# The convolution branch in four token-stationary groups: gate products made tokens first, turned by TensorE, taps channels first

## The chip, the core and the metric

The kernel runs on one core of a Trainium2 chip. The metric is the device time of one execution in microseconds; "before" is the median of three executions. Engines are named as in the profile: PE (TensorE, matmuls; PEld its weight loads), DVE (VectorE), ACT (ScalarE), POOL (GpSimd) and SP (SyncE, here a queue of DMAs alone).

## What is computed

One residual block over 512 tokens of width 2048: a projection of the normalised input into three branches (gated short convolution, latent attention, attention into a memory of 256 tokens) and merge gates, a projection of each branch, and an output projection. The change concerns the first branch:

```python
h = rms_norm(x, norm_g[l])
proj = h @ w_in[l]
(c_gate, b_gate, u, conv_z, ...) = jnp.split(proj, split_at, axis=-1)   # 1024 columns each
conv_y = b_gate * causal_depthwise_conv(c_gate * u, conv_w[l])          # 3 taps along the tokens
o_conv = (conv_y * jax.nn.silu(conv_z)) @ w_conv_out[l]
```

So 4096 of the columns of `w_in` make four arrays of 512 tokens by 1024 channels. Two are multiplied and filtered along the tokens, and the result is multiplied by the other two, one of them after SiLU. Everything is float32.

## The kernel before

**Matmuls.** Each float32 operand is cut into a high and a low part (`split`: ACT writes the high part, line 117, DVE the difference, line 119), and each product is three matmuls, high by high, high by low, low by high (`mm3`, lines 127 to 129). Large products are done by a two-by-two scheme with seven block products instead of eight, named P1 to P7 (P1, P7, P5, P6, P4, P3, P2 here); a step is one of these block products for one piece of the contraction. Sums and differences of weight blocks that a product needs are made by DVE in place in the loaded tile (`raw`, lines 306, 311, 366). The block forms of the input `BX` are made once and stay.

**Two kinds of group.** `f_group` holds 512 output columns with the weights stationary: PE loads a 128x128 block of weights and 256 tokens move through (128x256 rows in the profile). The result has channels on the partitions. A group has 14 steps of 24 matmuls. `t_group` holds 1024 output columns with the tokens stationary: 512 columns of weights move through (128x512 rows). The result has tokens on the partitions. A group has 28 steps of 12 matmuls. Both have 336 matmuls. `f_results` and `t_results` take the block products out of PSUM as they come and hand finished blocks on, for a `t_group` to `put(t, n, r)` (three of the four quarters; t the half of the tokens, n the half of the columns) and `direct` (the fourth, straight from PSUM, after P2).

**Order.** All groups append to one list, `steps`; `run_range` issues the matmuls of a step, then the forms (high and low parts) of the next step's weights, then what was hung behind the step with `after`. The order of instructions on PE, DVE, ACT and POOL is then set by a scheduler, within the dependencies; each engine runs its own list in order. SP's queue keeps the order written. Weights are loaded by `fetch` into a ring of ten tiles, up to eight loads ahead; high and low parts sit in a ring of six tiles (`wf`), so three steps' worth. Working tiles come from a pool of 19 (`q`), of which twelve hold block forms of the input through this stage. PSUM is two sets of four banks, `acc` and `aux`; a `t_group` uses all eight, X and W in `acc`, Y and Z in `aux`.

**The stage of the change.** One gate group (a `t_group` whose results go through a sigmoid and to DRAM), then eight `f_group`s for the convolution, each with 128 channels of all four arrays, then another gate group, four more `f_group`s, and so on. `conv_group` takes each group's results, channels on the partitions: DVE multiplies two (`cu`, L637), ACT makes the first tap (L639), DVE the others (L640, L641) and two more products (L642, L643), and the result is stored (L644). The tap weights are one number per channel, so here one per partition.

**Turning.** `transpose4` (L143) turns four 128x128 blocks by PE into one PSUM bank. In the last part of the program, `turn` does that for the merged rows.

Of the kernel before, what the change touches and what calls it, by code (L numbers as in the profile page):

```python
# [19 lines left out]
AF = mybir.ActivationFunctionType  # L20
# [3 lines left out]
P = 128  # L24
# [67 lines left out]
def body(ctx, tc, a, out):  # L92
# [70 lines left out]
    def g(col):  # L163
        return gains[:, col:col + 1]
# [30 lines left out]
    def q(name, dtype=F32):  # L195
        return work.tile([P, 2, 512], dtype, tag="q", name=name, bufs=NQ)
# [15 lines left out]
    def flat(t):  # L212
        return t.rearrange("p k n -> p (k n)")
# [405 lines left out]
                consume(0, sc["r0"])  # L619
        return results  # L620

    cus = []

    def conv_group(cb):
        keep = {}

        def consume(half, r):
            if not cus:
                cus.append(flat(q("cu"))[:, :S + 2])
                vec.memset(cus[0][:, :2], 0.0)  # L630
            cu = cus[0]
            if half:
                keep["bz"] = r
                act.activation(r[:, 1], r[:, 1], AF.Silu)
                return
            bz, cv = keep["bz"], r[:, 0]
            vec.tensor_tensor(out=cu[:, 2:], in0=r[:, 0], in1=r[:, 1], op=ALU.mult)  # L637
            wc = G_CONV + 3 * cb
            act.activation(cv, cu[:, 0:S], AF.Copy, scale=g(wc))  # L639
            vec.scalar_tensor_tensor(out=cv, in0=cu[:, 1:S + 1], scalar=g(wc + 1), in1=cv, op0=ALU.mult, op1=ALU.add)  # L640
            vec.scalar_tensor_tensor(out=cv, in0=cu[:, 2:S + 2], scalar=g(wc + 2), in1=cv, op0=ALU.mult, op1=ALU.add)  # L641
            vec.tensor_tensor(out=cv, in0=cv, in1=bz[:, 0], op=ALU.mult)  # L642
            vec.tensor_tensor(out=cv, in0=cv, in1=bz[:, 1], op=ALU.mult)  # L643
            nc.scalar.dma_start(adram[8 + cb], cv)  # L644
        return f_results(consume)

    def z_group(d, n0):
        def consume(half, r):
            act.activation(flat(r), flat(r), AF.Silu)
            nc.scalar.dma_start(two(d, n0 + 2 * half), r)  # L650
        return f_results(consume)

    def t_results(put, direct, early=None, add=None):


        sc, seen = {}, set()

        def results(name, bk):
            seen.add(name)
            if name in ("P1", "P7"):  # L660
                k, slot = ("u", "X") if name == "P1" else ("v", "Y")
                sc[k] = q(k)
                for tt in range(2):
                    act.activation(sc[k][:, tt], bk[slot][tt], AF.Copy)
                if early and name == "P7":
                    early(1, 1)
            u, v = sc.get("u"), sc.get("v")
            if name == "P5":
                for tt in range(2):
                    vec.tensor_tensor(out=v[:, tt], in0=bk["Z"][tt], in1=v[:, tt], op=ALU.add)  # L670
                if add:
                    vec.tensor_tensor(out=flat(v), in0=flat(v), in1=flat(add(1, 1)), op=ALU.add)
                if early:
                    early(0, 1)
            if name == "P6":
                for tt in range(2):
                    vec.tensor_tensor(out=u[:, tt], in0=bk["W"][tt], in1=u[:, tt], op=ALU.add)
                r = q("r")
                vec.tensor_tensor(out=flat(r), in0=flat(u), in1=flat(v), op=ALU.add)
                put(1, 1, r)  # L680
                if early:
                    early(1, 0)
            if name in ("P4", "P6") and seen >= {"P4", "P6"}:
                r = q("r")
                for tt in range(2):
                    vec.tensor_tensor(out=r[:, tt], in0=bk["Y"][tt], in1=u[:, tt], op=ALU.add)
                if add:
                    vec.tensor_tensor(out=flat(r), in0=flat(r), in1=flat(add(0, 1)), op=ALU.add)
                    vec.tensor_tensor(out=flat(u), in0=flat(u), in1=flat(add(1, 0)), op=ALU.add)
                put(0, 1, r)  # L690
                if early:
                    early(0, 0)
            if name == "P2":
                direct(bk["X"], q("r"))
            if name == "P3":
                r = q("r")
                for tt in range(2):
                    vec.tensor_tensor(out=r[:, tt], in0=bk["Z"][tt], in1=u[:, tt], op=ALU.add)
                put(1, 0, r)
        return results  # L700
# [21 lines left out]
    def gate_group(b, grp, lead=False):  # L722
        t_group(a[("w_gmem", "w_gconv", "w_gmla")[b]][grp], BX, rows_group(gdram[b], grp, AF.Sigmoid), lead)

    gate_group(0, 0, True)
    for cb in range(8):
        f_group(a["w_conv"][cb], BX, conv_group(cb), "aux" if cb % 2 else "acc")
    gate_group(0, 1)
    for grp in range(4):
        f_group(a["w_mlaz"][grp], BX, z_group(zdram, 4 * grp), "aux" if grp % 2 else "acc")  # L730
    gate_group(1, 0)
# [690 lines left out]
def two_by_two(w, cols, near=False):  # L1422

    w = np.concatenate([w[:, c0:c0 + n] for c0, n in cols], axis=1)
    if near:
        w = w.reshape(8, 2, P, 512).transpose(1, 0, 2, 3)
    w = w.reshape(2, 2, 4, P, 2, HS)
    w = np.stack([w[k, :, :, :, n] for k, n in ((0, 0), (0, 1), (1, 1), (1, 0))])  # L1430
    return np.ascontiguousarray(w.transpose(0, 1, 3, 2, 4)).reshape(8, P, 4 * HS)


def two_by_two_t(w, near=False):

    if near:
        w = w.reshape(8, 2, P, 1024).transpose(1, 0, 2, 3)
    w = w.reshape(2, 4, 2, P, 2, 512)  # L1440
    w = np.stack([w[k, :, :, :, n] for k, n in ((0, 0), (0, 1), (1, 1), (1, 0))])
    return np.ascontiguousarray(w.transpose(0, 1, 3, 2, 4)).reshape(16, P, KC * 512)
# [6 lines left out]
def layout(inp):  # L1449
    i = {k: np.asarray(v) for k, v in inp.items()}  # L1450
    w_in = i["w_in"][0]
    a = {}
    a["memT"] = np.ascontiguousarray(i["mem"][0].reshape(M, KB, P).transpose(2, 1, 0))
    a["xT"] = np.ascontiguousarray(i["x"][0].reshape(S, KB, P).transpose(2, 1, 0))
    a["pos"] = np.ascontiguousarray(i["positions"][0].reshape(NTB, P).T)
    cw = i["conv_w"][0].reshape(3, 8, P).transpose(2, 1, 0).reshape(P, 24)
    a["gains"] = np.ascontiguousarray(np.concatenate(
        [per_partition(i[n][0]) for n in ("norm_g", "mem_norm_g", "mla_q_norm_g", "mla_kv_norm_g",
                                          "mla_qn_nope_g", "mla_kn_nope_g", "mem_qn_g", "mem_kn_g")] + [cw],
        axis=1))  # L1460
    a["rgain"] = np.ascontiguousarray(np.broadcast_to(
        np.stack([i["mla_qn_rope_g"][0], i["mla_kn_rope_g"][0]])[None], (P, 2, 64)))
    a["ident"] = np.eye(P, dtype=np.float32)
    mask = np.zeros((P, S), np.float32)
    mask[:64, S - 64:] = NEG
    a["mask"] = mask
    a["invf"] = np.ascontiguousarray(np.broadcast_to(
        (10000.0 ** (-np.arange(32) / 32.0)).astype(np.float32)[None], (P, 32)))
    a["w_mem_kv"] = groups(i["w_mem_kv"][0], 0, 2048)
    a["w_cq"] = chunks(w_in, [(4096, 512)])  # L1470
    a["w_ckv0"] = chunks(w_in, [(4608, 288)])
    a["w_ckv1"] = chunks(w_in, [(4608 + 288, 288)])
    a["w_uq"] = groups(i["w_uq"][0], 0, 3072, 384)
    a["w_ukv"] = groups(i["w_ukv"][0], 0, 4096)
    a["w_memq"] = two_by_two_t(w_in[:, 7232:8256])[None]
    a["w_memz"] = np.stack([two_by_two(w_in, [(8256 + i * 512, 512)]) for i in range(2)])
    a["w_gmem"] = np.stack([two_by_two_t(w_in[:, 13376 + i * 1024:13376 + (i + 1) * 1024]) for i in range(2)])
    a["w_mem_out"] = groups(i["w_mem_out"][0], 0, 2048)
    a["w_conv"] = np.stack([two_by_two(w_in, [(c * 1024 + b * P, P) for c in (0, 2, 1, 3)]) for b in range(8)])
    a["w_gconv"] = np.stack([two_by_two_t(w_in[:, 9280 + i * 1024:9280 + (i + 1) * 1024]) for i in range(2)])  # L1480
    a["w_conv_out"] = groups(i["w_conv_out"][0], 0, 2048)
    a["w_mlaz"] = np.stack([two_by_two(w_in, [(5184 + i * 512, 512)]) for i in range(4)])
    a["w_gmla"] = np.stack([two_by_two_t(w_in[:, 11328 + i * 1024:11328 + (i + 1) * 1024]) for i in range(2)])
    a["w_mla_out"] = np.stack([two_by_two_t(i["w_mla_out"][0][:, k * 1024:(k + 1) * 1024]) for k in range(2)])
    a["w_o"] = np.stack([two_by_two_t(i["w_o"][0][:, k * 1024:(k + 1) * 1024], near=True) for k in range(2)])
    a["x"] = np.ascontiguousarray(i["x"][0].reshape(NTB, P, D))
    return a
# [12 lines left out]
```

## Time and profile before

| | before |
|---|---|
| median of 3 executions | 2132.38 us (2132.22 to 2133.94) |
| profiled execution | 2134.48 us |
| its span, first to last instruction | 2131.6 us |
| PE busy | 2098.9 us (98%), 12088 matmuls |
| DVE busy | 1638.2 us (77%) |
| ACT busy | 1059.1 us (50%) |
| weight loads for the convolution | 64 of 512 KB, issued from 156.1 to 454.4 us |
| DMA traffic | 330.41 MB, mean 155 GB/s |

Busy times count an engine as busy while at least one of its instructions runs. Matmuls overlap: a 128x512 row lasts 389 ns on average and the next one starts earlier, so the pace is read from the starts of neighbouring rows, or from how many lie in a stretch. A row of a group reads line, engine, operation, output<-inputs, shapes, count | busy us, mean ns of one | idle time before it and what ended that.

### The profile page before, as it was taken

Reading aid. Unit: us, or ns where it says so; the run is one execution under the profiler, and the core shown is the slowest. Engines: PE = TensorE matmul, PEld = TensorE weight load, DVE = VectorE, ACT = ScalarE, POOL = GpSimd, SP = SyncE. Lnnn points to the kernel's source line nnn. Section 1 sums busy time; section 2 is a strip of 40 time slices with the busy share of each in tenths; the row PEclk is TensorE's granted clock in tenths of the full one; section 3 lists DMA queues with packets and bytes.
Section 4 is the critical chain, followed back from the end, with each engine's and each line's share of the span. In section 5 each row is a group of like instructions: output and inputs, shape, how many; then the busy total and the mean of one; then the engine's idle time right before and its main releaser. Section 6 shows DMA issues by size and latency. Waiting matters only on the chain.

```text
span 2131.6 us, 31066 instructions
## 1 busy us (share of the span) xinstructions
PE 2098.9 (98%) x12088; PEld 1861.6 (87%) x12088; DVE 1638.2 (77%) x2169; ACT 1059.1 (50%) x1529; POOL 146.0 (7%) x183
## 2 busy tenths in 40 slices
PE   8999999999999999999999999999999999999999
PEld 8889999999899988898888888788888888888887
DVE  6976787788777777777778788767776688867986
ACT  5454444444444445444445576567665444434543
POOL 0000000000000000000000120312211201111000
PEclk9999999999999999999999999999999999999999
DMA  7345333324533445444446654312232667675572
GB/s 249 131 158 178 115 98 123 117 95 138 178 119 129 139 139 188 158 139 150 167 156 215 218 191 149 114 56 91 82 106 97 257 227 205 210 226 178 199 239 76
DMA packets 104147, 330.41 MB, mean 155 GB/s; under 512 B 10816, under 2 KB 11600, under 8 KB 104000
## 3 DMA queue, kind: packets, MB, share of 16 engines
q1 hardware_dynamic: 69488, 243.82, 34.6%
q0 software_dynamic: 13792, 45.57, 7.0%
q10 hardware_dynamic: 20720, 39.04, 4.8%
q8 instruction: 94, 1.54, 0.3%
q14 instruction: 53, 0.43, 0.1%
HBM read 284.22 MB, written 44.17 MB: 154 GB/s over the span
## 4 chain that ended last, share of the span: by engine, by line
PE 94%; DVE 3%; ACT 2%; issue 1%; DMA 1%; DVEq 0%; ACTq 0%; SPq 0%
PE aux L127 15%; PE aux L128 15%; PE aux L129 15%; PE acc L127 15%; PE acc L129 15%; PE acc L128 15%; PE aux L143 1%; DVE wlo L119 1%; PE aux L1213 1%; ACT whi L117 1%; PE aux L1196 0%; PE aux L1197 0%; PE aux L1195 0%; PE aux L1193 0%; PE aux L1194 0%
## 5 line engine op out<-in xcount | busy, mean ns | idle before, releaser
L117 ACT ACTIVATE whi<-raw 128x1024 fp32r<-128x1024 f32 (+2 forms) x598 | 621.6, 1041 | 817.0 <-PE aux L128 365.7
L119 DVE TENSOR_TENSOR wlo<-raw,whi 128x1024 fp32r<-128x1024 f32 (+2 forms) x598 | 713.9, 1199 | 325.6 <-ACT whi L117 321.2
L366 DVE TENSOR_TENSOR raw<-raw 128x1024 f32<-128x1024 f32 x176 | 214.9, 1222 | 11.3 <-DMA raw<-in_w_mla_out 3.0
L128 PE MATMUL aux<-wlo,f 128*128 128x512 f32 x352 | 137.1, 389 | 0.8 <-DVE wlo L119 0.8
L128 PE MATMUL acc<-wlo,b 128*128 128x512 f32 x352 | 137.0, 389 | 0.0
L129 PE MATMUL aux<-whi,f 128*128 128x512 f32 x352 | 137.0, 389 | 0.0
L129 PE MATMUL acc<-whi,b 128*128 128x512 f32 x352 | 137.0, 389 | 0.0
L129 PE MATMUL aux<-whi,b 128*128 128x512 f32 x352 | 137.0, 389 | 0.0
L128 PE MATMUL aux<-wlo,b 128*128 128x512 f32 x352 | 136.9, 389 | 0.0
L129 PE MATMUL acc<-b,wlo 128*128 128x256 f32 x448 | 126.8, 283 | 0.0
L127 PE MATMUL aux<-b,whi 128*128 128x256 f32 x448 | 126.8, 283 | 0.0
L128 PE MATMUL aux<-b,whi 128*128 128x256 f32 x448 | 126.8, 283 | 0.0
L129 PE MATMUL aux<-b,wlo 128*128 128x256 f32 x448 | 126.8, 283 | 0.0
L128 PE MATMUL acc<-b,whi 128*128 128x256 f32 x448 | 126.8, 283 | 0.0
L127 PE MATMUL acc<-b,whi 128*128 128x256 f32 x448 | 126.8, 283 | 0.0
L127 PE MATMUL acc<-whi,b 128*128 128x512 f32 x352 | 124.4, 390 | 0.1
L127 PE MATMUL aux<-whi,f 128*128 128x512 f32 x352 | 124.3, 389 | 0.0
L127 PE MATMUL aux<-whi,b 128*128 128x512 f32 x352 | 122.9, 390 | 0.5 <-ACT whi L117 0.5
L311 DVE TENSOR_TENSOR raw<-raw 128x1024 f32<-128x1024 f32 x84 | 102.4, 1222 | 1.7
L129 PE MATMUL acc<-f,wlo 128*128 128x256 f32 x336 | 95.4, 284 | 1.2 <-DVE wlo L119 1.2
L128 PE MATMUL acc<-f,whi 128*128 128x256 f32 x336 | 95.1, 283 | 0.0
L127 PE MATMUL aux<-f,whi 128*128 128x256 f32 x336 | 95.1, 283 | 0.0
(388 smaller groups left out, 5308.9 us busy)
## 6 DMA issues: line engine op xcount, KB each, us to landing
raw<-in_w_conv SPq DMA_DIRECT2D x64, 512.0 KB, 3.8
raw<-in_w_gmem SPq DMA_DIRECT2D x44, 512.0 KB, 3.3
raw<-in_w_mla_out SPq DMA_DIRECT2D x44, 512.0 KB, 4.8
raw<-in_w_o SPq DMA_DIRECT2D x44, 512.0 KB, 4.3
raw<-in_w_gconv SPq DMA_DIRECT2D x40, 512.0 KB, 3.6
raw<-in_w_gmla SPq DMA_DIRECT2D x40, 512.0 KB, 3.6
raw<-in_w_mlaz SPq DMA_DIRECT2D x32, 512.0 KB, 3.7
raw<-in_w_mem_kv SPq DMA_DIRECT2D x32, 512.0 KB, 4.2
```

Source lines behind the costliest of these rows:

```text
L117: act.activation(hi, src, AF.Copy, scale=1.0 if g is None else g)
L119: vec.tensor_tensor(out=lo, in0=src, in1=r32(hi), op=ALU.subtract)
L127: nc.tensor.matmul(o, lhsT=s[0], rhs=m[0], start=start, stop=False, skip_group_check=shared)
L128: nc.tensor.matmul(o, lhsT=s[0], rhs=m[1], start=False, stop=False, skip_group_check=shared)
L129: nc.tensor.matmul(o, lhsT=s[1], rhs=m[0], start=False, stop=stop, skip_group_check=shared)
L143: nc.tensor.transpose(out=b[:, i * P:(i + 1) * P], in_=s, identity=ident)
L311: vec.tensor_tensor(out=src_, in0=fetch(i0), in1=fetch(i1), op=op)
L366: vec.tensor_tensor(out=src_, in0=in0, in1=in1, op=op)
L1213: nc.tensor.transpose(out=b[:, i * P:(i + 1) * P], in_=ps[i][:, j * P:(j + 1) * P], identity=ident)
```

## The change

The eight `f_group`s become four `t_group`s of 1024 columns: for each half `h` of the channels, one with the columns of `c_gate` and `u`, one with those of `b_gate` and `conv_z`. The weights are packed anew on the host for this. `conv_rows` multiplies the two arrays of a group tokens first; the product stays in two working tiles (`keep`). When both groups of a half are through, `conv_turn` turns the two products for 128 channels at a time: four transposes into an `acc` bank, which ACT copies to `cu`, four into an `aux` bank, which DVE reads in the last product. Taps are as before. The turns hang behind steps 0, 2, 4 and 6 of the group that follows (in the second half that is the gate group).

```diff
-    def conv_group(cb):
-        keep = {}
-        def consume(half, r):
...
-            vec.tensor_tensor(out=cu[:, 2:], in0=r[:, 0], in1=r[:, 1], op=ALU.mult)
...
-            vec.tensor_tensor(out=cv, in0=cv, in1=bz[:, 0], op=ALU.mult)
-            vec.tensor_tensor(out=cv, in0=cv, in1=bz[:, 1], op=ALU.mult)
-            nc.scalar.dma_start(adram[8 + cb], cv)
-        return f_results(consume)
...
+    def conv_rows(h, second):
+        def put(t, n, r):
+            if n:
+                if second:
+                    act.activation(flat(r), flat(r), AF.Silu)
+                keep[second, t] = r
+            else:
+                k = keep[second, t]
+                vec.tensor_tensor(out=flat(k), in0=flat(r), in1=flat(k), op=ALU.mult)
+
+        def direct(x, r):
+            k = keep[second, 0]
+            for tt in range(2):
+                vec.tensor_tensor(out=k[:, tt], in0=x[tt], in1=k[:, tt], op=ALU.mult)
+        return t_results(put, direct, own=False)
+
+    def conv_turn(h, f):
+        if not cus:
+            for _ in range(2):
+                cus.append(flat(q("cu"))[:, :S + 2])
+                vec.memset(cus[-1][:, :2], 0.0)
+        cu = cus[f % 2]
+        rows = [[keep[n, i // 2][:, i % 2, f * P:(f + 1) * P] for i in range(NTB)] for n in range(2)]
+        b = transpose4(rows[0], "acc")
+        act.activation(cu[:, 2:], b, AF.Copy)
+        bz = transpose4(rows[1], "aux")
+        cv = q("cv")[:, 0]
+        wc = G_CONV + 3 * (4 * h + f)
+        act.activation(cv, cu[:, 0:S], AF.Copy, scale=g(wc))
+        vec.scalar_tensor_tensor(out=cv, in0=cu[:, 1:S + 1], scalar=g(wc + 1), in1=cv, op0=ALU.mult, op1=ALU.add)
+        vec.scalar_tensor_tensor(out=cv, in0=cu[:, 2:S + 2], scalar=g(wc + 2), in1=cv, op0=ALU.mult, op1=ALU.add)
+        vec.tensor_tensor(out=cv, in0=bz, in1=cv, op=ALU.mult)
+        nc.scalar.dma_start(adram[8 + 4 * h + f], cv)
...
-    for cb in range(8):
-        f_group(a["w_conv"][cb], BX, conv_group(cb), "aux" if cb % 2 else "acc")
+    later = []
+    for h in range(2):
+        for second in range(2):
+            t_group(a["w_conv"][2 * h + second], BX, conv_rows(h, second))
+        for f in range(4):
+            later.append((len(steps) + 2 * f, lambda h=h, f=f: conv_turn(h, f)))
     gate_group(0, 1)
+    for i, f in later:
+        after(i, f)
...
-    a["w_conv"] = np.stack([two_by_two(w_in, [(c * 1024 + b * P, P) for c in (0, 2, 1, 3)]) for b in range(8)])
+    a["w_conv"] = np.stack([two_by_two_t(np.concatenate([w_in[:, c * 1024 + h * 512:c * 1024 + h * 512 + 512] for c in cs], axis=1))
+                           for h in range(2) for cs in ((0, 2), (1, 3))])
```

(`own=False` keeps `t_results` from taking a tile for `direct`.) The scheduler then orders the instructions as follows. On PE, before, the first convolution group (`b` is a block form of the input, here the moving operand; PE's rows name the moving operand first):

```order
L127 MATMUL acc<-b_869,whi 128x256
L128 MATMUL acc<-b_870,whi 128x256
L129 MATMUL acc<-b_869,wlo 128x256
L127 MATMUL acc<-b_952,whi 128x256
L128 MATMUL acc<-b_953,whi 128x256
```

On PE, after, between the first P1 and P7 steps of the group behind the first half (`f` and `b_952` are block forms of the input, now stationary, `r` the kept products):

```order
L143 MATMUL acc<-ident,r 128x128 x4
L143 MATMUL aux<-ident,r 128x128
L127 MATMUL aux<-whi,f 128x512 x2
L143 MATMUL aux<-ident,r 128x128
L128 MATMUL aux<-wlo,f 128x512
...
L143 MATMUL aux<-ident,r 128x128 x3
L143 MATMUL acc<-ident,r 128x128 x4
L143 MATMUL aux<-ident,r 128x128 x3
L143 MATMUL acc<-ident,r 128x128 x4
L128 MATMUL acc<-wlo,b_952 128x512
```

The transposes stand in PE's list between matmuls of the following group, and those of `aux` wait for the product that DVE makes in `direct` and `put` (L717, L712).

On DVE, before, the tap work of one convolution group (L637 to L643) among the weights of the next:

```order
L637 TENSOR_TENSOR cu<-r_2952 128x512
L119 TENSOR_TENSOR wlo<-raw,whi 128x1024
L119 TENSOR_TENSOR wlo<-s,whi 128x1024
L640 SCALAR_TENSOR_TENSOR r_2952<-cu,gains,r_2952 128x512
L119 TENSOR_TENSOR wlo<-raw,whi 128x1024
L641 SCALAR_TENSOR_TENSOR r_2952<-cu,gains,r_2952 128x512
L311 TENSOR_TENSOR raw<-raw 128x1024
L642 TENSOR_TENSOR r_2952<-r_2952,r_2861 128x512
L119 TENSOR_TENSOR wlo<-raw,whi 128x1024
L643 TENSOR_TENSOR r_2952<-r_2952,r_2861 128x512
```

On DVE, after, the second and third turn of the first half, and the start of what follows:

```order
L119 TENSOR_TENSOR wlo<-raw,whi 128x1024 x2
L733 SCALAR_TENSOR_TENSOR cv<-cu,gains,cv 128x512
L366 TENSOR_TENSOR raw<-raw 128x1024
L733 SCALAR_TENSOR_TENSOR cv<-cu,gains,cv 128x512
L734 SCALAR_TENSOR_TENSOR cv<-cu,gains,cv 128x512
L366 TENSOR_TENSOR raw<-raw 128x1024
L734 SCALAR_TENSOR_TENSOR cv<-cu,gains,cv 128x512
L119 TENSOR_TENSOR wlo<-raw,whi 128x1024
L735 TENSOR_TENSOR cv<-aux,cv 128x512
L119 TENSOR_TENSOR wlo<-raw,whi 128x1024
L735 TENSOR_TENSOR cv<-aux,cv 128x512
L366 TENSOR_TENSOR raw<-raw 128x1024 x2
```

What stood once per group of 14 steps now stands four times within eight steps, between the weights (`wlo`) that these steps need.

On ACT, after, the last turns of the second half (L728 copies a turned bank to `cu`, L732 is the first tap, L736 the store, L639 takes P1's and P7's banks):

```order
L728 ACTIVATE cu<-acc 128x512
L732 ACTIVATE cv<-cu,gains 128x512
L736 DMA adram<-cv 128x512 x2
L117 ACTIVATE whi<-raw 128x1024
L639 ACTIVATE u<-acc 128x512
L732 ACTIVATE cv<-cu,gains 128x512
L117 ACTIVATE whi<-raw 128x1024
```

The last row makes the high part of the first P5 weights, and it now stands behind two stores and two copies.

More of the change, by code (lines that the diff above doesn't have):

```diff
@@ L620, in f_results @@
         return results
-    cus = []
-    def conv_group(cb):
-        keep = {}
-        def consume(half, r):
[L628 to L641, printed above, removed]
-            vec.tensor_tensor(out=cv, in0=cv, in1=bz[:, 0], op=ALU.mult)
-            vec.tensor_tensor(out=cv, in0=cv, in1=bz[:, 1], op=ALU.mult)
-            nc.scalar.dma_start(adram[8 + cb], cv)
-        return f_results(consume)
     def z_group(d, n0):
@@ L651, in z_group, with t_results @@
         return f_results(consume)
-    def t_results(put, direct, early=None, add=None):
+    def t_results(put, direct, early=None, add=None, own=True):
         sc, seen = {}, set()
@@ L693, in results @@
             if name == "P2":
-                direct(bk["X"], q("r"))
+                direct(bk["X"], q("r") if own else None)
             if name == "P3":
@@ L723, in gate_group @@
         t_group(a[("w_gmem", "w_gconv", "w_gmla")[b]][grp], BX, rows_group(gdram[b], grp, AF.Sigmoid), lead)
-    gate_group(0, 0, True)
-    for cb in range(8):
-        f_group(a["w_conv"][cb], BX, conv_group(cb), "aux" if cb % 2 else "acc")
+    cus = []
+    keep = {}
+    def conv_rows(h, second):
[29 more added lines that the diff above has]
+        nc.scalar.dma_start(adram[8 + 4 * h + f], cv)
+    gate_group(0, 0, True)
+    later = []
[4 more added lines that the diff above has]
+            later.append((len(steps) + 2 * f, lambda h=h, f=f: conv_turn(h, f)))
     gate_group(0, 1)
+    for i, f in later:
+        after(i, f)
     for grp in range(4):
```

## The prediction

> **What bounds the kernel now.** I read the page first (busy shares, granted clock, the chain of waits), then PE's waits around the convolution stage, then a table of stages, then single instructions.
>
> ```profile
> span 2131.6 us, 31066 instructions
> PE 2098.9 (98%) x12088; PEld 1861.6 (87%) x12088; DVE 1638.2 (77%) x2169; ACT 1059.1 (50%) x1529; POOL 146.0 (7%) x183
> PEclk9999999999999999999999999999999999999999
> PE 94%; DVE 3%; ACT 2%; issue 1%; DMA 1%; DVEq 0%; ACTq 0%; SPq 0%
> PE acc L129 <- DVE wlo L119: 0.4, 1, 0.4
> ```
>
> PE is busy for 98% of the span and holds 94% of the chain that ends last. The last row is the whole list of PE's waits between 170 and 520 us, the stretch that holds the convolution groups: one wait of 0.4 us. So here the time is what PE's instructions take, and a change pays or costs through their number and spacing, until some engine that feeds PE comes late.
>
> ```profile
> core 0: us, PE busy (x) PEld busy (x) DVE busy (x) ACT busy (x) POOL busy (x), PEclk, DMA share, GB/s
> 183.43:506.62 323.19, 322.80 (x2689) 322.59 (x2688) 256.40 (x254) 141.93 (x153) 0.00 (x0) 1.00 0.36 114
> 506.62:582.81 76.19, 76.19 (x339) 63.07 (x337) 60.54 (x58) 36.58 (x38) 0.00 (x0) 1.00 0.46 156
> 744.73:897.08 152.35, 152.35 (x675) 126.13 (x674) 116.75 (x106) 72.61 (x75) 0.00 (x0) 1.00 0.50 163
> 820.91:842.67 21.76, 19.45 (x17) 1.00 0.46 149
> ```
>
> The first row is the eight convolution groups, from their first 256-column matmul to the first 512-column one after them: 323.19 us for 8 x 336 = 2688 matmuls. The second is one token-stationary group (the gate group behind them), the third two such groups back to back (the gates of the convolution branch): 76.19 and 76.18 us for 336 matmuls each. The fourth is DVE alone in the first eight steps (P1 and P7) of the second of those two groups: 19.45 of 21.76 us busy. The clock is 1.00 in all of them.
>
> **The change part by part.**
>
> *Fewer, wider matmuls.* Eight groups of 336 matmuls of 256 columns become four groups of 336 of 512 columns. By stages that is 323.19 - 4 x 76.18 = 18.5 us. The single rows agree:
>
> ```profile
> 256.90 0.28 PE L128 MATMUL aux<-b,whi 128*128 128x256 f32 x1
> 257.02 0.28 PE L129 MATMUL aux<-b,wlo 128*128 128x256 f32 x1
> 46.52 0.30 PE L127 MATMUL acc<-whi,xhi 128*128 128x288 f32 x1
> 46.65 0.30 PE L128 MATMUL acc<-wlo,xhi 128*128 128x288 f32 x1
> 46.78 0.60 PE L143 MATMUL aux<-ident,rows 128*128 128x128 f32 x4
> 47.35 0.30 PE L127 MATMUL acc<-whi,xhi 128*128 128x288 f32 x1
> 153.06 0.39 PE L128 MATMUL aux<-wlo,f 128*128 128x512 f32 x1
> 153.28 0.39 PE L129 MATMUL aux<-whi,f 128*128 128x512 f32 x1
> 1905.90 1.03 PE L143 MATMUL acc<-ident,m 128*128 128x128 f32 x8
> 1907.01 0.39 PE L129 MATMUL aux<-whi,actl 128*128 128x512 f32 x1
> ```
>
> Starts lie 0.120 us apart at 256 columns, about 0.133 at 288 and, over a group, 76.18 / 336 = 0.2267 at 512. From 256 to 512 that is 0.417 ns a column, which leaves 13 ns per matmul that do not depend on the width; 1344 matmuls fewer save 1344 x 13.3 ns = 17.9 us, and the 0.4 us of waiting at the stage's start makes most of the rest. I take 18.4. Bounds: 17.9 (that wait comes back somewhere) and 18.5. The Trainium skill, "TensorE: Matmul & The Clock Gate", section "Back-to-back issue gap", speaks against this: it gives N / 2.4 + 2.5 ns between isolated matmuls, 109 ns at 256 columns and 216 ns at 512, so that two narrow ones cost nearly what one wide one does, and the stage would save an estimated 2688 x 0.1092 - 1344 x 0.2158 = 3.5 us instead of 18.4; with the other two terms below the change would then be an estimated 9 us slower. The rows above (120 and 227 ns) do not bear it out.
>
> *64 transposes on PE.* Each of eight turns transposes four blocks of the first product and four of the second. Four of them move the next-but-one matmul by 47.35 - 46.78 - 0.133 = 0.44 us, eight near the end of the program by 1907.01 - 1905.90 - 0.227 = 0.88: 0.11 us each, with nothing extra per insertion. 64 x 0.11 = 7.1 us, all on PE's path. Bounds: 4.3 (128 columns at 0.417 ns plus the 13 ns) and 7.7 (the 0.120 us of a 256-column matmul each); I take the 0.11, the same operation, and keep the ends.
>
> So PE's own work falls by 18.4 - 7.1 = 11.3 us. The rest is whether PE is fed in time.
>
> *DVE around the turns.* Averaged, DVE is no tighter than today (256.40 of 323.19 us; in a token group 58.4 of 76.18). But what a convolution group spread over its own steps now stands at a few places. Durations:
>
> ```profile
> L641 DVE SCALAR_TENSOR_TENSOR r<-cu,gains,r 128x512 f32<-128x512 f32 x8 | 6.0, 746 | 0.0
> L643 DVE TENSOR_TENSOR r<-r,r 128x512 f32<-128x512 f32 x8 | 5.5, 682 | 0.0
> L639 ACT ACTIVATE r<-cu,gains 128x512 f32<-128x512 f32 x8 | 5.8, 726 | 3.2 <-DVE cu L637 3.2
> L1354 ACT ACTIVATE E<-acc 128x512 f32<-128x512 f32 x4 | 2.4, 601 | 3.3 <-PE acc L143 3.3
> ```
>
> After each pair of groups DVE has the two products of `direct` (0.6 us apart), the one of `put` (1.14) and four turns of two scalar-tensor-tensors and one product. By the order this all stands between the end of the pair and the weights of the first P5 step, within the eight steps of P1 and P7, which are DVE's tightest. What those eight steps look like today, at the boundary of the two gate groups of the third stage row:
>
> ```profile
> 817.68 0.68 DVE L698 TENSOR_TENSOR r<-aux,u 128x512 f32<-128x512 f32 x1
> 818.28 1.22 DVE L366 TENSOR_TENSOR raw<-raw 128x1024 f32<-128x1024 f32 x1
> 819.42 0.68 DVE L698 TENSOR_TENSOR r<-aux,u 128x512 f32<-128x512 f32 x1
> 821.15 1.22 DVE L119 TENSOR_TENSOR wlo<-raw,whi 128x1024 fp32r<-128x1024 f32 x1
> 826.74 2.36 DVE L119 TENSOR_TENSOR wlo<-raw,whi 128x1024 fp32r<-128x1024 f32 x2
> 829.13 2.48 DVE L366 TENSOR_TENSOR raw<-raw 128x1024 f32<-128x1024 f32 x2
> 841.16 1.22 DVE L119 TENSOR_TENSOR wlo<-raw,whi 128x1024 fp32r<-128x1024 f32 x1
> 843.13 0.39 PE L128 MATMUL aux<-wlo,b 128*128 128x512 f32 x1
> ```
>
> The row at 841.16 makes the low part of the first P5 weights, and PE reads it at 843.13. From 821.15 through that row DVE has 16 instructions of 1024 elements; they follow each other at 1.14 to 1.20 us (818.28 to 819.42; 826.74 to 829.13 for two), 16 x 1.17 = 18.7. Added: 2 x 0.6 + 1.14 = 2.3 ahead of them, and 11 of the 12 turn instructions (the last product stands behind that row in the new order) at 0.65 each, that is 7.2 (rows of 0.746 and 0.682 less the 0.08 by which neighbours overlap, as 0.68 is followed after 0.60 at 817.68). Without any gap DVE would finish at 821.15 + 18.7 + 2.3 + 7.2 = 849.4. PE would ask for it at 843.13 + 32 x 0.11 = 846.7. The difference, 2.7 us, is PE waiting, for each of the two halves. I add 0.1 for hand-overs: 2 x 2.8 = 5.6 us. Bounds: nothing (DVE's gaps shrink further and the weights in the ring cover it), and 2 x (2.3 + 7.8 - 3.5) = 13.2 us (all added DVE work exposed, less the time PE is busy with transposes).
>
> Behind the eight steps DVE has room again, so the lag does not carry over.
>
> *ACT, queues, memory.* ACT gets a copy out of PSUM (0.60) per turn beside the scaled copy (0.726) that it has today; at half load (36.58 of 76.19 us) it is no bound on average. But its queue is in order and in front of the next weights' high parts stand the stores of `cv`, which wait for DVE's last product: a part of the same lag, not another one. In the half whose turns fall into the gate group, the order puts the first P5 high part behind two copies (0.60 + 0.73), so up to 1.3 us more could show there; it is inside the bounds.
>
> ```profile
> raw<-in_w_conv SPq DMA_DIRECT2D x64, 512.0 KB, 3.8
> adram<-r ACTq DMA_DIRECT2D x8, 256.0 KB, 4.7
> 1960.00:2000.00 40.00, 39.97 (x184) 33.10 (x184) 38.68 (x42) 19.40 (x23) 2.17 (x3) 1.00 0.66 227
> ```
>
> SP issues 80 loads of 512 KB for these weights instead of 64, 8.4 MB more, in a stage whose DMA share is 0.36; the other token groups run at 0.46 to 0.50 with PE full, so I cost it at nothing (cover: eight loads ahead, 3.8 us each, against 2.7 us a step). The eight stores stay; a `cv` tile is free only 4.7 us after its store starts, shorter than the 5.4 us from turn to turn.
>
> **Sum.** -18.4 + 7.1 + 5.6 = -5.7 us. The profiled execution took 2134.48 us (2131.6 of span), so 2128.8 for it; the median of the three runs is 2132.38, 2.1 lower, and the forecast for the median is 2132.4 - 5.7 = 2126.7 us.
>
> **The rivals.**
> 1. *The cover holds, no lag.* For: in the row 1960 to 2000, DVE is busy 38.68 of 40 us and PE still 39.97. Against: the count above exceeds DVE's time outright. Time: 2132.4 - 11.3 = 2121.1.
> 2. *Nothing is covered.* DVE's in-order queue exposes all it is given: -11.3 + 13.2 = +1.9, 2134.3. For: the eight steps have 2.3 us of free DVE time only (21.76 - 19.45).
> 3. *A convoy, slower.* Each turn is a round trip: transposes 0.44, copy 0.60, scaled copy 0.726, two scalar-tensor-tensors 1.49, product 0.68, 3.9 us in all; the next turn needs the PSUM bank that the product frees, and PE's transposes stand in PE's queue ahead of matmuls that are ready. Fully exposed 8 x 3.9 = 31 us: 2132.4 - 11.3 + 31 = 2152. It eats the gain from 11.3 / 8 = 1.4 us a turn and is slower from 2 us a turn. Against: the order puts ten or more matmuls (2.3 us) between most of them.
> 4. *The wide matmuls save nothing*, because the 13 ns go with columns, not instructions: two narrow starts, 0.240, for each wide one. Then +7.1 + 5.6 - 0.5 = +12.2, 2144.6. Against: three token groups timed here. The rule of the Trainium skill quoted above is nearest to this rival.
>
> **How the numbers follow.** No change means within 0.2%, 4.3 us, about what a measurement of this kernel can tell. Forecast (lag of 2 to 9 us, its own range 2123 to 2130): 0.60. Rival 1: 0.17, rival 2: 0.13, rival 3: 0.07, rival 4: 0.03. Faster by over 4.3 needs a lag below 7.0: rival 1 and 0.42 of the forecast's 0.60, 0.59. Within: 0.18 + 0.13 = 0.31. Slower: 0.10. The range reaches from rival 1 to most of rival 2: 2121.5 to 2133.
>
> **What would show it.** Convolution stage to the end of the gate group: 5 x 76.18 + 7.1 + 5.6 = 394 us where it was 399.4 (323.19 + 76.19). PE's waits on `wlo` (and `whi`), 2 to 4 us in each of two stretches of about 25 us right behind the second and fourth convolution group, none elsewhere. Transposes 0.11 us apart. DVE over 95% busy in those stretches. I am wrong if the token groups take other than 76.2 us without turns, if waits lie outside those two stretches, or if PE waits on banks (transposes waiting for DVE's product) rather than on weights.

## The result, and the profile after

The changed kernel takes 2125.99 us (median of six runs, 2124.97 to 2128.29) where the kernel before takes 2133.60 (six runs, 2132.22 to 2135.05): a ratio of 0.9965, with a 95% interval of 0.9954 to 0.9975, so about 7.6 us faster. The forecast was 2126.7, 5.7 us faster. The first lines of the page, for the profiled execution (2125.74 us), with the chain and the loads of these weights:

```profile
span 2124.0 us, 28553 instructions
PE 2089.1 (98%) x10808; PEld 1797.2 (85%) x10808; DVE 1637.6 (77%) x2162; ACT 1058.5 (50%) x1525; POOL 146.0 (7%) x183
...
PE 93%; DVE 3%; ACT 2%; issue 1%; DMA 1%; SPq 0%; ACTq 0%; DVEq 0%
...
raw<-in_w_conv SPq DMA_DIRECT2D x80, 512.0 KB, 4.1
```

There are 1280 PE instructions fewer (1344 matmuls gone, 64 transposes come), and PE's busy share is 98% as before: the kernel has the same bound and less of it. The stages, by the table of windows (us, then busy time and count of PE, PEld, DVE, ACT, POOL, then clock, DMA share and GB/s). The rows are the first two convolution groups, the second two with the turns of the first half, and the gate group with the turns of the second half:

```profile
183.32:335.64 152.32, 152.32 (x673) 126.17 (x672) 119.44 (x111) 68.13 (x70) 0.00 (x0) 1.00 0.47 145
335.64:492.87 157.23, 156.67 (x706) 129.20 (x704) 128.81 (x126) 69.33 (x74) 0.00 (x0) 1.00 0.45 141
492.87:575.84 82.97, 80.89 (x370) 66.06 (x369) 68.14 (x69) 39.97 (x44) 0.00 (x0) 1.00 0.48 152
sum 392.52, PE 389.88 PEld 321.43 DVE 316.38 ACT 177.43 POOL 0.00; mean PE 129.96 PEld 107.14 DVE 105.46 ACT 59.14 POOL 0.00
```

The sum row is the stage of which the rest speaks: 392.52 us, where the same work took 399.38 before (183.43 to 582.81). That is 6.9 of the 7.6 us of the span; the stage starts 0.1 earlier, and what follows it is 0.6 shorter. The first row is two token groups without turns: 152.32 / 2 = 76.16 us each. The other two are longer than their two groups and one group by 4.9 and 6.8 us: transposes and waiting. PE's list of waits from 183 to 600 us names who came late:

```profile
PE aux L127 <- ACT whi L117: 0.9, 1, 0.9
PE aux L128 <- DVE wlo L119: 0.9, 2, 0.5
PE acc L127 <- ACT whi L117: 0.7, 1, 0.7
PE acc L129 <- DVE wlo L119: 0.4, 1, 0.4
```

The last row lies behind the stage, at the first 256-column group; the kernel before has such a wait at its first one. The other three, 2.5 us, are all in the two stretches behind the second and the fourth group. PE loses more there than they say:

```profile
352.86 0.61 PE L127 MATMUL acc<-whi,b 128*128 128x512 f32 x2
353.94 0.50 PE L128 MATMUL aux<-wlo,f 128*128 128x512 f32 x1 [0.47 <-DVE wlo L119]
354.28 0.40 PE L129 MATMUL aux<-whi,f 128*128 128x512 f32 x1
```

Two matmuls from 352.86 on should be followed at 352.86 + 2 x 0.2267 = 353.31; the next starts at 353.94, so 0.63 late and not 0.47, since the list counts from the modelled end of the matmul before (0.16 us past the point where the next could start). The one after it comes 0.34 behind, not 0.227. So the list finds the place of a wait, and its size is read from the stage against one that has no wait (see no_taps and padded_spread below): 392.52 - 388.3 = 4.2 us.

### The profile page after: what moved, and what is told of

The parts are those of the page before. It is cut to its first block, busy times and chain, and to the rows that moved or that the text cites. A ratio compares the mean times of both kernels' runs of the same rounds, so it can differ in the third digit from the quotient of the medians.

```text
span 2124.0 us, 28553 instructions
## 1 busy us (share of the span) xinstructions
PE 2089.1 (98%) x10808; PEld 1797.2 (85%) x10808; DVE 1637.6 (77%) x2162; ACT 1058.5 (50%) x1525; POOL 146.0 (7%) x183
## 4 chain that ended last, share of the span: by engine, by line
PE 93%; DVE 3%; ACT 2%; issue 1%; DMA 1%; SPq 0%; ACTq 0%; DVEq 0%
PE aux L128 15%; PE aux L127 15%; PE aux L129 15%; PE acc L127 14%; PE acc L128 14%; PE acc L129 14%; PE aux L143 1%; DVE wlo L119 1%; ACT whi L117 1%; PE aux L1232 1%; PE aux L1214 0%; PE aux L1212 0%; PE aux L1213 0%; PE aux L1215 0%; PE aux L1216 0%
## 5 line engine op out<-in xcount | busy, mean ns | idle before, releaser
L119 DVE TENSOR_TENSOR wlo<-raw,whi 128x1024 fp32r<-128x1024 f32 (+2 forms) x614 | 733.2, 1200 | 325.3 <-ACT whi L117 320.2
L366 DVE TENSOR_TENSOR raw<-raw 128x1024 f32<-128x1024 f32 x240 | 293.3, 1223 | 11.5 <-DMA raw<-in_w_mla_out 2.8
L129 PE MATMUL aux<-whi,f 128*128 128x512 f32 x480 | 186.9, 389 | 0.0
L129 PE MATMUL acc<-whi,b 128*128 128x512 f32 x480 | 186.8, 389 | 0.0
L129 PE MATMUL aux<-whi,b 128*128 128x512 f32 x480 | 186.8, 389 | 0.0
L127 PE MATMUL aux<-whi,f 128*128 128x512 f32 x480 | 170.2, 390 | 0.0
L127 PE MATMUL acc<-whi,b 128*128 128x512 f32 x480 | 169.0, 390 | 0.8 <-ACT whi L117 0.7
L127 PE MATMUL aux<-whi,b 128*128 128x512 f32 x480 | 168.1, 390 | 1.4 <-ACT whi L117 1.4
L128 PEld LDWEIGHTS aux<-wlo,f 128*128 128x128 f32 x480 | 90.1, 188 | 21.2 <-DVE wlo L119 2.5
L127 PEld LDWEIGHTS aux<-whi,b 128*128 128x128 f32 x480 | 90.0, 188 | 20.8 <-ACT whi L117 2.3
L127 PEld LDWEIGHTS acc<-whi,b 128*128 128x128 f32 x480 | 89.8, 188 | 20.0 <-ACT whi L117 1.6
L128 PEld LDWEIGHTS aux<-wlo,b 128*128 128x128 f32 x480 | 90.1, 188 | 18.8 <-DVE wlo L119 0.2
L129 PEld LDWEIGHTS aux<-whi,b 128*128 128x128 f32 x480 | 90.1, 188 | 18.7
L128 PEld LDWEIGHTS acc<-wlo,b 128*128 128x128 f32 x480 | 90.1, 188 | 18.7 <-DVE wlo L119 0.2
L129 PEld LDWEIGHTS aux<-whi,f 128*128 128x128 f32 x480 | 90.2, 188 | 18.6
L129 PEld LDWEIGHTS acc<-whi,b 128*128 128x128 f32 x480 | 90.1, 188 | 18.5
L127 PEld LDWEIGHTS aux<-whi,f 128*128 128x128 f32 x480 | 89.9, 188 | 18.8 <-ACT E L1373 0.3
L128 PE MATMUL acc<-wlo,f 128*128 128x512 f32 x240 | 93.4, 389 | 0.0
```

Source lines behind the costliest of these rows:

```text
L119: vec.tensor_tensor(out=lo, in0=src, in1=r32(hi), op=ALU.subtract)
L127: nc.tensor.matmul(o, lhsT=s[0], rhs=m[0], start=start, stop=False, skip_group_check=shared)
L128: nc.tensor.matmul(o, lhsT=s[0], rhs=m[1], start=False, stop=False, skip_group_check=shared)
L129: nc.tensor.matmul(o, lhsT=s[1], rhs=m[0], start=False, stop=stop, skip_group_check=shared)
L366: vec.tensor_tensor(out=src_, in0=in0, in1=in1, op=op)
```

## The experiments

All stages below run from the first matmul of the convolution groups to the end of the gate group. Each is read from one profiled execution; of two kernels there are two such executions, and their stages agree (392.52 and 392.51 us for the changed kernel, 388.41 twice for spread3). The first two convolution groups take 152.32 us in each of them but narrow and one_tile_more, so the quoted rows are the second two groups and the gate group.

**no_turn_no_taps: nothing but five groups.**

```
-        if not cus: ...            (transposes, copy, taps, product)
+        cv = flat(keep[f % 2, f // 2])[:, :S]
         nc.scalar.dma_start(adram[8 + 4 * h + f], cv)
```

> Left out: the transposes and the taps; slices of the token-first products are stored in their place. Stage = from the first matmul of the convolution groups to the end of the gate group behind them; in the changed kernel 392.52 us (183.32 to 575.84) = 5 x 76.16 + 64 x 0.11 of transposes + 4.7 of waiting (1.4 in the first half, 3.3 in the second). My theory: what is left is five token groups, 380.8 us, and no wait, for DVE's 2.3 us of gate products per pair fits into the free time of the eight steps. Rival (the wide groups themselves, or the gate products, carry waits): 382 to 385.

```profile
183.04:335.36 152.32, 152.32 (x673) 126.17 (x672) 119.43 (x110) 68.11 (x70) 0.00 (x0) 1.00 0.47 149
335.36:487.68 152.32, 152.32 (x673) 126.17 (x672) 121.53 (x113) 65.03 (x66) 0.00 (x0) 1.00 0.46 145
487.68:563.84 76.16, 76.16 (x337) 63.08 (x336) 60.74 (x57) 35.23 (x36) 0.00 (x0) 1.00 0.49 159
```

380.80 us, five times 76.16 with PE busy throughout. So the wide groups alone are worth 399.38 - 380.80 = 18.6 us, and the turns with their consequences cost 392.52 - 380.80 = 11.7. The gate products alone (121.53 of DVE against 119.43) make no wait.

**no_taps and more_dve: less and more work for DVE.** The first leaves the two scalar-tensor-tensors out (8 instructions per half), the second adds two instructions of the same kind and size behind each product. As written they take the maximum of a value with itself, so, other than the expectation says, the values stay as they are.

```
-        vec.scalar_tensor_tensor(out=cv, in0=cu[:, 1:S + 1], ...)      (no_taps)
-        vec.scalar_tensor_tensor(out=cv, in0=cu[:, 2:S + 2], ...)
...
+        for _ in range(2):                                             (more_dve)
+            vec.scalar_tensor_tensor(out=cv, in0=cv, scalar=1.0, in1=cv, op0=ALU.mult, op1=ALU.max)
```

> Left out: the second and third tap, that is the two scalar-tensor-tensors of each turn, 16 x 0.65 = 5.2 us of DVE per half; transposes, PSUM copy, scaled copy and product stay. Theory A (DVE late): the waits go in the first half (1.4 < 5.2), and in the second to 0 to 1.3, what ACT's order alone makes: stage 387.8 to 389.1. Rival (the waits are ACT's order, or the round trip of a turn): the waits on the high parts stay, stage 390.5 to 392.5.

> Added: two more DVE instructions of 128x512 per turn behind the product (they change the result), 16 x 0.65 = 10.4 us in both halves together. Theory A (DVE has no room left ahead of the deadline): PE's waits grow by nearly all of it that stands ahead of the deadline, 4 to 5.2 us per half, stage 400 to 403. Rival (DVE still has gaps, the waits are ACT's or the round trip's): plus 0 to 3, 392.5 to 395.5.

Rows of no_taps, then of more_dve:

```profile
335.69:491.67 155.98, 155.98 (x705) 129.41 (x704) 123.99 (x118) 70.10 (x74) 0.00 (x0) 1.00 0.46 142
491.67:571.69 80.02, 80.02 (x369) 66.16 (x368) 63.20 (x61) 40.17 (x44) 0.00 (x0) 1.00 0.50 158
```

```profile
336.14:498.01 161.87, 158.96 (x705) 130.10 (x704) 133.25 (x134) 69.51 (x74) 0.00 (x0) 0.99 0.43 137
498.01:585.50 87.49, 82.76 (x369) 67.06 (x368) 72.85 (x77) 39.82 (x44) 0.00 (x0) 0.98 0.45 144
...
PE aux L127 <- DVE cv L735: 1.9, 1, 1.9
```

no_taps: 152.32 + 155.98 + 80.02 = 388.32 us, PE without a gap; both halves lose their waits. What is left over five groups is the transposes: (388.32 - 380.80) / 64 = 0.117 us each. more_dve: 401.68, which is 9.16 more than the changed kernel, for 9.15 us more of DVE busy time (133.25 + 72.85 against 128.81 + 68.14). In these stretches each microsecond more of DVE is a microsecond of the kernel; less of it gains only the waits that there are (no_taps takes 9.8 us of DVE away and gains 4.2). That is the theory of a late DVE; ACT, whose work is nearly the same in all three, is not what bounds. The last row, of more_dve's list of waits, is the only one of PE for a turn's product in these runs: the convoy of rival 3 shows once, where DVE has more to do than the change gives it.

**no_turn: the transposes alone left out.**

```
-        b = transpose4(rows[0], "acc")
-        act.activation(cu[:, 2:], b, AF.Copy)
-        bz = transpose4(rows[1], "aux")
+        rows = [flat(keep[n, f // 2])[:, (f % 2) * S:(f % 2 + 1) * S] for n in range(2)]
+        act.activation(cu[:, 2:], rows[0], AF.Copy)
+        bz = rows[1]
```

> Left out: the 64 transposes alone (the taps and the product run on the token-first rows, so DVE and ACT keep all their instructions). Theory A, a deadline: DVE is the bound of the eight steps behind each pair, and the transposes are time in which it catches up. Taking 3.5 us of PE away per half then only lets PE arrive 3.5 us earlier and wait longer: waits grow from 4.7 to about 10 to 11.7 us, stage 390.5 to 392.5. Theory B, two separate terms as in my sum: the transposes' 7.0 us go and the waits stay, stage 385.5.

```profile
335.55:492.23 156.68, 154.81 (x674) 126.91 (x673) 128.81 (x126) 69.97 (x76) 0.00 (x0) 0.99 0.45 141
492.23:573.12 80.89, 78.44 (x338) 63.89 (x336) 67.81 (x69) 38.24 (x42) 0.00 (x0) 0.98 0.48 156
```

The stage is 389.89 us: 7.5 us of transposes taken out of PE give 2.6 back. The waits are 4.4 and 4.7 us, 9.1 together instead of 4.2. Just under theory A's range and far from theory B's 385.5: the two terms of the sum are not separate. While DVE is late, a transpose is time in which it catches up. The halves differ in what they gave back: 0.55 us in the first (157.23 to 156.68) and 2.08 in the second (82.97 to 80.89). The second half lost something else too, a gap of 2.55 us on DVE that is explained below and that this kernel does not have. So the first half is the cleaner reading: of 3.7 us of transposes, 0.55 came back.

**narrow: half the width in the same groups.**

```
-                    mm3(bk[slot][tt], x..., (hi[:, kt], lo[:, kt]), ...)
+                    for n in range(2):
+                        m = slice(n * HS, (n + 1) * HS)
+                        mm3(bk[slot][tt][:, m], x..., (hi[:, kt, m], lo[:, kt, m]), ...)
```

> Each 512-column matmul of the four convolution groups becomes two of 256 columns of the same stationary block; all else as in the changed kernel. My theory (13.3 ns per matmul, whatever its width): 1344 matmuls more, 17.9 us, less up to 1.3 that the longer steps give back of the first half's wait: stage 409 to 410.5 where it is 392.5. Rival 4 of the prediction (two narrow ones cost what one wide one does, and the old groups were slower for another reason, such as which operand is stationary): 392.5.

```profile
183.62 0.28 PE L128 MATMUL acc<-wlo,b 128*128 128x256 f32 x1
183.74 0.28 PE L129 MATMUL acc<-whi,b 128*128 128x256 f32 x1
...
183.39:593.13 409.74, 407.23 (x3090) 392.13 (x3089) 317.92 (x304) 177.84 (x188) 0.00 (x0) 1.00 0.42 139
```

0.120 us apart with the tokens stationary too, and 409.74 - 392.52 = 17.2 us longer: 17.9 less 0.7 that the first half's wait gives back. The fixed part goes with the instruction, whichever operand is stationary. (Each matmul here has its own weight load, and the loads of the 256-column streams fill nearly all of the time, 392.13 of 409.74 us here and 322.59 of 323.19 before; so the runs don't tell a fixed part of the matmul from one of its load.) By the formula for isolated matmuls in the Trainium skill, "TensorE: Matmul & The Clock Gate", section "Back-to-back issue gap", N / 2.4 + 2.5 ns, this edit would cost an estimated 1344 x 2.5 ns = 3.4 us. The section itself does not offer it for streams, though the prediction set it against its own term, and the measured 17.2 shows that it does not carry over to this one.

**Why the second half waits longer.** The first half waits 1.2 us (157.23 against 155.98 to 156.06 without waits), the second 3.0 (82.97 against 79.92 to 80.02). The two rows of PE's list on `whi` are both in the second half, and they read as if ACT were late. ACT's own timeline in the second half says otherwise, and DVE's, the last row, shows where it begins:

```profile
508.04 1.07 ACT L117 ACTIVATE whi<-raw 128x1024 fp32r<-128x1024 f32 x1 [4.00 <-DVE raw L366]
515.76 1.06 ACT L117 ACTIVATE whi<-raw 128x1024 fp32r<-128x1024 f32 x1 [4.13 <-DVE raw L366]
```

```profile
501.93 1.29 DVE L673 TENSOR_TENSOR r<-aux,u 128x512 f32<-128x512 f32 x2 [2.55 <-PE acc L143]
```

ACT stood idle for 4 us each time until DVE had made the difference of two weight blocks (L366). An earlier ACT alone would also have gained PE little: right behind the longest of these waits PE needs a `wlo` that DVE has only just finished (517.99 + 1.22 = 519.21):

```profile
517.99 1.22 DVE L119 TENSOR_TENSOR wlo<-raw,whi 128x1024 fp32r<-128x1024 f32 x1
...
518.92 0.49 PE L127 MATMUL aux<-whi,b 128*128 128x512 f32 x1 [0.95 <-ACT whi L117]
...
519.26 0.50 PE L128 MATMUL aux<-wlo,f 128*128 128x512 f32 x1
```

DVE itself stood still for 2.55 us in front of the result of P3 (the row at 501.93), for transposes that it does not read. In the two halves the same result stands at different places of DVE's queue; first half above, second below (rows numbered by their place; L673 is P3's result, L717 and L712 the products of the gates, L733 the first tap):

```
188 L673 TENSOR_TENSOR r<-aux,u 128x512
189 L366 TENSOR_TENSOR raw<-raw 128x1024
190 L717 TENSOR_TENSOR r<-acc,r 128x512
191 L712 TENSOR_TENSOR r<-r 128x1024
...
196 L733 SCALAR_TENSOR_TENSOR cv<-cu,gains,cv 128x512
...
286 L673 TENSOR_TENSOR r<-aux,u 128x512 x2
287 L119 TENSOR_TENSOR wlo<-raw,whi 128x1024
288 L733 SCALAR_TENSOR_TENSOR cv<-cu,gains,cv 128x512
289 L712 TENSOR_TENSOR r<-r 128x1024
```

The two padded tiles `cu` are taken from pool `q` at the first turn and kept. From then on two of its 19 tiles are missing, P3's `r` has no buffer until the transposes have read the first product (in the program it takes over one of that product's two), and DVE, in order, waits with it. Three kernels test this.

```
-    NQ, NB1, NW, NF = 19, 8, 10, 6                                     (one_tile_more)
+    NQ, NB1, NW, NF = 20, 8, 9, 6
...
-            for _ in range(2): cus.append(...)        cu = cus[f % 2]  (one_padded)
+            cus.append(...)                           cu = cus[0]
...
-        act.activation(cu[:, 2:], b, AF.Copy)                          (direct)
-        act.activation(cv, cu[:, 0:S], AF.Copy, scale=g(wc)) ...
+        act.activation(cv, b, AF.Copy, scale=g(wc + 2))
+        vec.scalar_tensor_tensor(out=cv[:, 1:], in0=b[:, :S - 1], scalar=g(wc + 1), in1=cv[:, 1:], ...)
+        vec.scalar_tensor_tensor(out=cv[:, 2:], in0=b[:, :S - 2], scalar=g(wc), in1=cv[:, 2:], ...)
```

> One tile more in the pool that holds the rows and one fewer in the ring of raw weights (20 and 9 for 19 and 10). Theory: the second half waits 2.95 us where the first waits 1.25, because from the first half on the two padded tiles hold two buffers of that pool; the result tile of P3 then gets a buffer only when the transposes have read the first product, and DVE's queue stands still for 2.55 us. With one more tile the order of the second half is that of the first, its wait falls to 1.25, stage 390.8, kernel 1.7 us below the changed one (about 2124.3). Rival (the second half is slower because of what follows it, the gate group's own ACT and DVE work, or because ACT's copies stand ahead of the high parts): stage stays 392.5.

> The taps read the transposed block in PSUM instead of a padded copy: no copy by ACT (0.60 us a turn), one hand-over less, two tiles fewer in use; DVE's work stays. Theory (DVE late; a tile short in the second half): first half about as now, 1.0 to 1.3, second half as the first: stage 390.3 to 390.8. Rival (ACT's copies ahead of the high parts make the waits): nearly all 4.2 us of waiting go, stage 388.3 to 389.

> One padded tile instead of two, nothing else: ACT still copies every block, and one tile of the pool is free again. Theory (the second half's surplus of waiting, 2.95 against 1.25, is the tile that P3's result lacks): both halves alike, 1.25 to 2 each, since one padded tile also makes the turns queue for each other; stage 390.8 to 392, second half no worse than the first. Rival (in the kernel direct it was the missing ACT copies that made the second half shorter): the second half stays 1.7 us above the first, stage 392.5 or more.

Rows of one_padded, then of direct, then of one_tile_more:

```profile
335.12:491.57 156.45, 156.40 (x706) 129.26 (x705) 128.50 (x125) 69.39 (x74) 0.00 (x0) 1.00 0.44 142
491.57:571.85 80.28, 80.23 (x369) 66.19 (x368) 67.67 (x69) 39.61 (x44) 0.00 (x0) 1.00 0.48 157
```

```profile
335.52:492.33 156.81, 156.49 (x705) 129.19 (x704) 128.85 (x125) 67.21 (x70) 0.00 (x0) 1.00 0.44 141
492.33:572.96 80.63, 80.33 (x369) 66.11 (x368) 68.04 (x69) 37.41 (x40) 0.00 (x0) 1.00 0.48 157
```

```profile
336.63:495.95 159.32, 157.57 (x705) 129.05 (x704) 128.53 (x125) 69.28 (x74) 0.00 (x0) 1.00 0.44 139
495.95:580.58 84.63, 81.99 (x369) 67.42 (x368) 68.04 (x69) 39.70 (x44) 0.00 (x0) 0.98 0.46 149
...
PE aux L128 <- DVE wlo L119: 16.6, 17, 5.2
```

one_padded, with every ACT copy kept, waits 0.4 us in each half (stage 389.05, 2124.37 us in its one run), and direct 0.7 in each (389.76, 2124.09, ratio 0.9954 with 0.9941 to 0.9966). In both P3's result stands in front of the turns and the 2.55 us gap is gone; so ACT's copies did not make the second half's surplus, and the missing tile is what is left. no_turn agrees: it keeps both padded tiles and every ACT copy, but there the tile does not wait for transposes, P3's result stands in front of the turns (490.73), and the halves wait alike (4.4 and 4.7). A kernel that frees a tile and changes nothing else is missing. For the stage, direct lies between its two forecasts and one_padded below both. Both were better than forecast in the first half too (0.4 and 0.7 where 1.2 stood): with one padded tile no turn's first tap stands ahead of the previous turn's product in DVE's queue any more, and in direct DVE stops for ACT in front of a first tap once, for 0.17 us (0.26 and 0.34 in the first half of the changed kernel). Which of these gives how much was not tried by itself. one_tile_more missed: the order of the second half is that of the first, but the tile came from the ring of raw weights, and nine there are too few. Over the whole program PE waits 16.6 us in the row on `wlo` shown (1.1 in the changed kernel), the first two groups, without any turn, already take 154.17 us instead of 152.32, the stage is 398.12, and the kernel is slower than the one before: 2144.36 us, ratio 1.0048 with 1.0035 to 1.0060. It says nothing on the question.

**spread3 and padded_spread: the turns further apart.** Edit on top of direct and of one_padded:

```
-        bz = transpose4(rows[1], "aux")
+        bz = transpose4(rows[1], "acc")
...
-            later.append((len(steps) + 2 * f, ...))
+            later.append((len(steps) + 3 * f, ...))
```

> As direct, and the four turns of a half stand three steps apart instead of two (at steps 0, 3, 6 and 9 of the next group), both blocks in banks of the other tag. Theory (DVE late at the first P5 weights): at most three turns stand ahead of that point, 2.1 us less for DVE, and the waits fall below 0.5 us: stage 388.3 to 388.8, kernel 3.7 to 4.2 below the changed one, 2122. Rival (the waits move to the later steps, which are as tight, or PE waits for the two banks that are left): stage 390.5 to 393.

> As one_padded, with the turns three steps apart and both blocks in banks of one tag: the spacing of spread3 with ACT's copies kept. Theory (the spacing does it): waits below 0.5, stage 388.3 to 388.9. Rival (reading the taps from PSUM did it): stage 390.5 or more.

> The changed kernel itself, timed beside spread3 on one chip: 0.9965 of the kernel before, 7 to 8 us below it.

> The kernel spread3 beside the changed one on the same chip. Theory: 4.1 us below the changed kernel, what its stage is shorter by (388.4 against 392.5), so 0.9945 of the kernel before. Rival (its 2120.8 us came from the rest of the program): no difference in the stage's part, 0.996 to 0.997.

Rows of padded_spread, then of spread3_again:

```profile
335.61:491.67 156.06, 156.06 (x706) 129.31 (x704) 128.41 (x125) 69.53 (x74) 0.00 (x0) 1.00 0.44 142
491.67:571.59 79.92, 79.92 (x369) 66.25 (x368) 67.57 (x69) 39.73 (x44) 0.00 (x0) 1.00 0.48 158
```

```profile
335.21:491.32 156.11, 156.11 (x706) 129.26 (x704) 128.65 (x125) 67.23 (x70) 0.00 (x0) 1.00 0.44 142
491.32:571.30 79.98, 79.98 (x370) 66.20 (x368) 67.85 (x69) 37.43 (x40) 0.00 (x0) 1.00 0.47 158
```

PE has no gap left in either (388.30 and 388.41 us), with DVE's busy time as in the changed kernel (196.0 and 196.5 us against 196.95). The spacing is not what gained most of that. Against the kernels that these two are built on, the stage is 0.75 us shorter (389.05 to 388.30) and 1.35 (389.76 to 388.41), for two changes at once that were not tried separately: turns 8 us apart instead of 5.4, and both blocks in banks of one tag. The larger part of the 4.2 and 4.1 us against the changed kernel, 3.5 and 2.8, had come with one padded tile fewer and with none. The wider spacing with two padded tiles was not tried. spread3 took 2120.84 us (ratio 0.9940, 0.9926 to 0.9953); timed beside the changed kernel on one chip 2121.78 (0.9942, 0.9927 to 0.9956) against 2125.80 (0.9962, 0.9949 to 0.9975): 4.0 us, the stage's 4.1. padded_spread took 2120.39 in one run. Both took less than the kernel before and the changed one.

## Why the prediction was right, point by point

- *Fewer, wider matmuls, -18.4.* Measured 18.6 (399.38 - 380.80), and 17.2 when undone alone by narrow. Rival 4 is out.
- *64 transposes, +7.1.* 7.5 where DVE is on time (0.117 us each, where 0.11 was read; inside the bounds of 4.3 and 7.7). The lower bound, a price by columns, was wrong: 128 columns cost nearly what 256 do (0.120).
- *DVE around the turns, +5.6.* 4.2, inside the bounds, in the two stretches named and through the operands named (`wlo` and `whi`, no bank). The mechanism was right, but not the one place: the prediction has PE wait at the first P5 weights, and PE waits from the sixth of the eight steps on (the rows at 353.94 and 512.19 are of P7). The sign "2 to 4 us in each" failed in the first half (1.2). DVE was busy 24.69 of the 25.36 us behind the second group, as the sign says; behind the fourth, all of the 20.77 us after its gap, but with the gap 27.2 of 29.83, which is 91% and not over 95%:

```profile
335.64:361.00 25.36, 24.80 (x124) 20.15 (x123) 24.69 (x29) 12.76 (x18) 0.00 (x0) 1.00 0.32 94
...
499.38:501.93 2.55, 2.55 (x18) 2.14 (x16) 0.00 (x1) 1.06 (x1) 0.00 (x0) 1.00 0.54 164
501.93:522.70 20.77, 18.69 (x87) 14.47 (x86) 20.77 (x24) 11.25 (x16) 0.00 (x0) 1.00 0.30 95
```

- *2.8 in each half* is the term that was mis-sized, and that the sum came near is luck. The step that failed is "16 instructions of 1024 elements": the row at 841.16 is not the one that the matmul at 843.13 reads. Each step has one low part (L119), in the order of the steps. The first step's is the row at 816.54, since the next one ends only after PE's first `wlo` matmul has started (821.37). So the ninth, of the first P5 step, is the row at 838.75, and the program's buffers say the same. The kernel before:

```profile
816.54 1.23 DVE L119 TENSOR_TENSOR wlo<-raw,whi 128x1024 fp32r<-128x1024 f32 x1 [1.49 <-ACT whi L117]
821.37 0.39 PE L128 MATMUL acc<-wlo,b 128*128 128x512 f32 x1
...
838.75 1.23 DVE L119 TENSOR_TENSOR wlo<-raw,whi 128x1024 fp32r<-128x1024 f32 x1 [0.54 <-ACT whi L117]
```

  And the changed kernel, first half, the same weights and their reader:

```profile
361.13 1.22 DVE L119 TENSOR_TENSOR wlo<-raw,whi 128x1024 fp32r<-128x1024 f32 x1
362.45 0.46 PE L128 MATMUL aux<-wlo,b 128*128 128x512 f32 x1
```

  That makes 14 instructions in both kernels and 2.3 us less: 847.0 against 846.7, so the prediction's own count gives a wait of 0.3 us a half. What it left out is DVE standing still: in the first half 0.26 and 0.34 us in front of taps, for ACT's copy (0.9 with the 0.3; measured 1.2), in the second the 2.55 us for a tile (2.85 with the 0.3; measured 3.0). The pool was never counted. So two instructions too many stood in for gaps that the count left out. That these terms add up in each half is an estimate; in the second the order of DVE's rows differs in more than the gap.
- *ACT's order, up to 1.3 in the second half*: not the cause, although the waits on `whi` are listed there and one of them (518.92) is on P5's first high part, behind two copies as foreseen. ACT had waited for DVE, and PE's next `wlo` came no earlier (519.26).
- *Adding the terms.* no_turn shows that the transposes and the lag are not independent: taken out alone, the transposes are worth 2.6, not 7.5, and part of the 2.6 is the tile's gap. In the sum they met at the right values because the lag was worked out with the 32 transposes in PE's clock (846.7 for 843.13).
- *Loads and stores, nothing.* Right: 80 loads land in a median of 4.1 us (3.8 before), and PE waits on none of them.
- *The total.* Forecast -5.7, measured -7.6: 1.4 from the lag, 0.2 from the matmuls, less 0.4 on the transposes, and 0.7 outside the stage, which no step of the prediction names. It is no more than that part differs between two executions of one program: after_again has the same span of 2124.0 us, and its stage, as long, ends at 574.89 instead of 575.84. The time itself came within 0.7 us of the forecast (2125.99 against 2126.7) because the median of the kernel before over six runs is 1.2 us above that of the three that the forecast starts from; in the change it is 1.9 off.

Rival 1 (no lag) was false for this kernel, and its time, 2121.1, is that of spread3: the cover is there with one padded tile or none and the turns a step further apart. Rival 2 (13.2 us of waiting) is out by the 4.2. Rival 3 did not come up: PE's list for the stage of the changed kernel has no wait for a bank or for a product.

## What to carry to other kernels

Work that is small on an engine's average can cost its full price where it is bunched: compare the engine's free time in the very steps it lands in, and look for what makes it stand still there. Here a tile given back was worth more (3.5 us of the stage, with the new order of the taps) than wider spacing on top of it (0.75). When an in-order engine stands still for something that it does not read, look for a buffer it wants to write; tiles taken once and kept can make the second pass through a loop different from the first. A wait charged to one engine is followed back one more step before that engine is blamed.

## What had not been expected of the hardware

A transpose of a 128x128 float block cost 0.117 us in a stream of matmuls (7.5 us for 64, in two kernels without waits), as much as a 256-column matmul (0.120), though the law that fits 256, 288 and 512 columns (0.417 ns a column and 13 ns) would give 0.067. Whether the weight load that goes with each of them sets that floor, or the type (the transposes are plain float32, the matmuls fp32r), was not tried. And a late weight costs PE more than the idle time shown: 0.47 us listed was 0.63 by the starts, and the next matmul stood 0.34 behind instead of 0.227.
